# RWKV state step: three products in one PSUM bank, carried states copied by ACT and DVE

## The chip, the cores and the metric

The kernel runs on one core of one Trainium2 chip. The metric is device time in microseconds of one launch. A core has engines that run side by side, each with its own list of instructions, tied by semaphores: TensorE (PE, with its weight loads shown apart as PEld), VectorE (DVE), ScalarE (ACT), GpSimd (POOL) and SyncE (SP, which here only issues transfers). PE writes its products into PSUM; DVE and ACT read them from there; POOL works on SBUF here.

## The reference, cut to what matters

The program is one layer of a hybrid backbone: adaLN modulation, one input projection, then side by side multi-head latent attention (8 heads) and bidirectional RWKV-7 time mixing (16 heads of 64), one output projection, a post norm, and a SwiGLU FFN with its own post norm. 640 tokens: one prompt of 128 and one sample of 512. The part that the change touches is the scan of RWKV, one per direction and head:

```
def step(S, inp):
    r_t, w_t, k_t, v_t, kk_t, a_t = inp
    sa = jnp.einsum("bhvk,bhk->bhv", S, -kk_t)
    S = S * w_t[:, :, None, :] + sa[..., None] * (kk_t * a_t)[:, :, None, :] \
        + v_t[..., None] * k_t[:, :, None, :]
    return S, jnp.einsum("bhvk,bhk->bhv", S, r_t)
s_fin, ys = lax.scan(step, s0, (to_t(r), to_t(decay), to_t(k), to_t(v), to_t(kk), to_t(a)), reverse=reverse)
```

The state S (64 x 64) of every head is carried through the tokens; ys is the output, s_fin of the prompt a result of its own.

## The kernel before, in words

**The scan in chunks.** The tokens are cut into ten chunks of 64 (C = 64). Inside a chunk the recurrence is solved by a small triangular inverse, and only the states at the chunks' borders are carried. Heads go in 8 pairs (index i), both directions d at once (forward, and backward with the order of the tokens reversed), and the ten chunks in two halves j of five. For one pair and half the steps are `rwkv_prep` (factors such as nk and pr), `rwkv_grams` (products of these, m<-pr,nk, copied by ACT to mab and mrb and by DVE to pr), `inverse` (in its middle t<-m,tc of line 617, its transpose u of line 619, and the copies pm and uf of lines 630 to 632 between the products m<-t,mab and m<-u,pm), and `rwkv_chain`. Beside the inverse and the chain run the decays of the other half or the next pair (m<-xa,lw and others; products nk, ta, ks on DVE), the finishing of the pair before (m<-sg,gw onto y), and all the time the big input projection, whose products acc<-xh,whi fill PE's gaps.

**One step of the chain** (e = 0 to 4, 80 in all). px, four small products of the states sv with pr; ACT copies them to xs (line 873); POOL makes sd, the decayed states (line 883); the outputs of the step before are written into two banks and copied (ACT) or added (DVE) into y; psg, four products of xs with the inverse; ACT and DVE copy its two head halves to zv (lines 894 and 895); pn, up to four products of zv with bk; and on DVE up to four scalar-tensor-tensor operations (lines 905 and 906) that make the next state from pn, dc and sd. At the end of the first half the state that goes on is written to cy ("carry"); the second half starts with a copy of it into its own sv, on POOL (line 845), beside two memsets (lines 843 and 846).

**PSUM.** `mps()` gives a tile of one bank with the tag "m"; three banks rotate under that tag for all the work named above. One bank ("x") is for the modulation, and two tiles of two banks ("acc") for the projection.

**Order.** PE's order in this part is the order in which `Jobs` steps through the generators: each `yield HOP[...]` gives a planned delay from a table, and `Tensor.matmul` counts a cost for each product. Banks and the other engines' instructions don't enter into it. The orders of DVE, ACT and POOL are laid out by a scheduler over the whole program. After 1500 us come the output projection and the FFN (products b<-op,qh, b<-p,qh and others; weights are split into a rounded part qh by ACT, line 1302, and the rest ql by DVE), and in the last part, too, the scheduler decides PE's order.

Of the kernel before, what the change touches and what calls it, by code (L numbers as in the profile page):

```python
# [27 lines left out]
C = 64  # L28
# [130 lines left out]
def step_kernel(ctx: ExitStack, tc: tile.TileContext, a: dict, o: dict, upto: int = 99, npairs: int = NPAIR, dbg=None):  # L159
    nc = tc.nc  # L160
    HOP = dict(HOPS[0])
    V, A, G, DMA = nc.vector, nc.scalar, nc.gpsimd, nc.sync
# [11 lines left out]
    def nm(s):  # L174
        uid[0] += 1
        return f"{s}_{uid[0]}"
# [7 lines left out]
    def rtile(name, n, tag, bufs, dtype=F32):  # L184
        return rp.tile([P, n], dtype, tag=tag, name=nm(name), bufs=bufs)

    def slot(name, dtype=F32):
        return rtile(name, NT, "s", N_S, dtype)
# [16 lines left out]
    def mps():  # L205
        return m_ps.tile([P, 512], F32, tag="m", name=nm("m"))
# [19 lines left out]
    def tt(eng, out, x, y, op):  # L226
        eng.tensor_tensor(out=out, in0=x, in1=y, op=op)  # L227
# [7 lines left out]
    def stt(out, x, s, y, op0, op1):  # L235
        V.scalar_tensor_tensor(out=out, in0=x, scalar=s, in1=y, op0=op0, op1=op1)  # L236
# [295 lines left out]
    def rows(h):  # L532
        return slice(64 * h, 64 * h + 64)
# [4 lines left out]
    def cc(e):  # L538
        return slice(e * C, e * C + C)
# [136 lines left out]
    def nat(d, j):  # L676

        h = j if d == 0 else 1 - j
        return slice(h * HN, h * HN + HN)
# [145 lines left out]
    def rwkv_chain(i, j, sh, u):  # L825

        sv_, zv, bk, mrb, pr, dc, cy = u["sv"], u["zv"], u["bk"], u["mrb"], u["pr"], u["dc"], sh["carry"]

        def lanes(t, h, e):

            return t[rows(h), e: e + 6: 5, h, :]

        def lane2(t, h):
            return t[rows(h), :2 * C].rearrange("p (d v) -> p d v", v=C)

        if j == 0:
            sh["fs"] = rtile("fs", 2 * C, "fs", 2)
            sh["y"] = slot("y")
        for h in range(2):
            if j == 0:  # L840
                for d, e in ((0, 0), (1, 7)):
                    DMA.dma_start(out=sv_[rows(h), e, h, :], in_=a["states"][d, i, rows(h)])
                G.memset(sv_[rows(h), 5, h, :], 0.0)
            else:
                G.tensor_copy(lanes(sv_, h, 0), lane2(cy, h))
                G.memset(sv_[rows(h), 3, h, :], 0.0)
        y = sh["y"]

        def outputs(c):


            pss = [mps()[:, :C] for _ in range(2)]
            ms = (slice(0, C), slice(None, None, -1))
            for d, ps in enumerate(pss):
                for h in range(2):
                    T.matmul(ps[rows(h)], sv_[:, 5 * d + c, h, :], pr[h][:, 5 * d + c, 1, :][:, ms[d]], start=True, stop=False)
            for d, ps in enumerate(pss):
                for h in range(2):
                    T.matmul(ps[rows(h)], zv[rows(h), 5 * d + c, h, :], mrb[rows(h), 5 * d + c, :][:, ms[d]], start=False, stop=True)
            for d in range(2):  # L860
                yc = y[:, nat(d, j)][:, cc(c if d == 0 else 4 - c)]
                if j == 0:
                    A.copy(yc, pss[d])
                else:
                    tt(V, yc, pss[d], yc, ALU.add)

        for e in range(5):
            px = mps()
            for d in range(2):
                for h in range(2):  # L870
                    T.matmul(px[rows(h), cc(d)], pr[h][:, 5 * d + e, 0, :], sv_[:, 5 * d + e, h, :], start=True, stop=True)
            xs = rtile("xs", 2 * C, "xs", 2)
            A.copy(xs, px[:, :2 * C])

            to = [AFTER[j, d][e] for d in range(2)]
            ds = [d for d in range(2) if to[d]]
            n = len(ds)
            es = slice(5 * ds[0] + e, 5 * ds[-1] + e + 1, 5)
            dv = slice(ds[0] * C, ds[-1] * C + C)
            sd = rtile("sd", 2 * C, "xs", 2)  # L880
            for h in range(2):
                rh = rows(h)
                tt(G, sd[rh, dv].rearrange("p (d v) -> p d v", v=C), sv_[rh, es, h, :],
                   dc[rh, es].unsqueeze(2).broadcast_to([C, n, C]), ALU.mult)

            if e:
                outputs(e - 1)
            else:
                yield HOP["x"]
            psg = mps()  # L890
            for d in range(2):
                for h in range(2):
                    T.matmul(psg[rows(h), cc(d)], u["u"][rows(h), cc(5 * d + e)], xs[rows(h), cc(d)], start=True, stop=True)
            A.copy(lanes(zv, 0, e), lane2(psg, 0))
            V.tensor_copy(lanes(zv, 1, e), lane2(psg, 1))
            yield HOP["s"]
            pn = mps()
            for d in ds:
                for h in range(2):
                    T.matmul(pn[rows(h), cc(d)], bk[:, 5 * d + e, h, :], zv[:, 5 * d + e, h, :], start=True, stop=True)  # L900
            for h in range(2):
                rh = rows(h)
                for d in ds:
                    q = 5 * d + e
                    dst = sv_[rh, q + 1, h, :] if to[d] == "next" else (cy if to[d] == "carry" else sh["fs"])[rh, cc(d)]
                    stt(dst, pn[rh, cc(d)], dc[rh, q: q + 1], sd[rh, cc(d)], ALU.mult, ALU.add)
            if e < 4:
                yield HOP["p"]
        outputs(4)
        if j == 1:  # L910
            DMA.dma_start(out=o["states"][i], in_=sh["fs"])
# [41 lines left out]
    def rwkv():  # L953
# [19 lines left out]
        for i in range(npairs):  # L973
            for j in range(2):
                yield from rwkv_prep(i, j, sh, u)
                yield from rwkv_grams(u)
                turned = jobs.spawn(rwkv_turned(i, j, sh, u), TURN)
                side = jobs.spawn(beside_second(i, sh) if j else beside_first(i, sh, last), RANK_S)
                u["u"] = yield from inverse(u["mab"])
                yield turned  # L980
                yield from rwkv_chain(i, j, sh, u)
                last = (i, sh)
                yield side
                if side.result:
                    sh, u = side.result
# [305 lines left out]
    def bank():  # L1291
        return b_ps.tile([P, 512], F32, tag="b", name=nm("b"))
# [359 lines left out]
    for n in range(2):  # L1652
        if n:
            ms[0].clear()
        for f in range(KT):
# [9 lines left out]
            ps = bank()  # L1665
# [358 lines left out]
```

## Time and profile before

| what | value |
|---|---|
| time, median of 3 runs | 3491.99 us (3489.88 to 3497.54) |
| profiled execution | 3500.31 us, its span 3498.5 us |
| mean granted clock of TensorE | 0.964 |
| PE busy | 3255.5 us (93%) |
| DVE busy | 2555.3 us (73%) |
| ACT busy | 1480.9 us (42%) |
| POOL busy | 1070.4 us (31%) |

Busy times are sums over the span of one execution. All times of rows further down are from that execution, and are to be set against its 3500.31 us, not against the median. The granted clock is the share of full speed that the throttle left to TensorE: 1.00 in a stretch is 2.4 GHz throughout, 0.50 is 1.2 GHz.

### The profile page before, as it was taken

Reading aid. Unit: us, or ns where it says so; the run is one execution under the profiler, and the core shown is the slowest. Engines: PE = TensorE matmul, PEld = TensorE weight load, DVE = VectorE, ACT = ScalarE, POOL = GpSimd, SP = SyncE. Lnnn points to the kernel's source line nnn. Section 1 sums busy time; section 2 is a strip of 40 time slices with the busy share of each in tenths; the row PEclk is TensorE's granted clock in tenths of the full one; section 3 lists DMA queues with packets and bytes.
Section 4 is the critical chain, followed back from the end, with each engine's and each line's share of the span. In section 5 each row is a group of like instructions: output and inputs, shape, how many; then the busy total and the mean of one; then the engine's idle time right before and its main releaser. Section 6 shows DMA issues by size and latency. Waiting matters only on the chain. (4 is left out here: it accounts for less than half of the span.)

```text
span 3498.5 us, 71287 instructions
## 1 busy us (share of the span) xinstructions
PE 3255.5 (93%) x27538; PEld 2961.4 (85%) x27538; DVE 2555.3 (73%) x4562; ACT 1480.9 (42%) x3115; POOL 1070.4 (31%) x1106
## 2 busy tenths in 40 slices
PE   7988998999999689999979999999999999999987
PEld 4677676777877578899979999999999999999886
DVE  1356766776766676468688888888888888778798
ACT  1144443443443454455454444444444444334334
POOL 0021222122122132102164444444444442212245
PEclk9998999999999899999999999999999999999997
DMA  8754444444211211085434443444443478776743
GB/s 300 240 175 137 142 147 139 161 160 139 66 61 59 72 34 36 31 270 179 142 116 144 155 136 127 134 132 138 133 128 125 144 252 293 255 250 207 256 128 108
DMA packets 289717, 529.06 MB, mean 151 GB/s; under 512 B 31008, under 2 KB 83680, under 8 KB 289376
## 3 DMA queue, kind: packets, MB, share of 16 engines
q1 hardware_dynamic: 289376, 524.49, 45.3%
q8 instruction: 216, 3.54, 0.4%
q14 instruction: 125, 1.02, 0.1%
HBM read 429.65 MB, written 93.09 MB: 149 GB/s over the span
## 5 line engine op out<-in xcount | busy, mean ns | idle before, releaser
L227 DVE TENSOR_TENSOR ql<-raw,qh 128x512 fp32r<-128x512 f32 (+1 forms) x1136 | 930.6, 833 | 263.6 <-ACT qh L1302 242.5
L1302 ACT CAST qh<-raw 128x512 fp32r<-128x512 f32 (+1 forms) x1136 | 660.2, 588 | 913.2 <-PE b L113 777.8
L227 POOL TENSOR_TENSOR raw<-raw,raw 128x512 f32<-128x512 f32 (+1 forms) x288 | 394.4, 1371 | 849.6 <-DVE ql L227 662.2
L113 PE MATMUL b<-t,qh 128*128 128x320 f32 x2816 | 621.7, 310 | 8.6 <-ACT qh L1302 7.3
L113 PE MATMUL b<-op,qh 128*128 128x320 f32 x2464 | 545.9, 315 | 18.2 <-DMA op<-hd 18.0
L113 PEld LDWEIGHTS b<-t,qh 128*128 128x128 f32 x2816 | 471.5, 188 | 10.1 <-ACT qh L1302 8.1
L113 PE MATMUL b<-p,qh 128*128 128x320 f32 x2112 | 468.2, 310 | 0.0
L113 PE MATMUL b<-t,ql 128*128 128x320 f32 x1408 | 435.3, 310 | 6.4 <-DVE ql L227 6.2
L113 PEld LDWEIGHTS b<-op,qh 128*128 128x128 f32 x2464 | 417.9, 192 | 24.6 <-issue 12.3
L113 PE MATMUL b<-op,ql 128*128 128x320 f32 x1232 | 375.3, 316 | 20.1 <-DVE ql L227 20.0
L113 PEld LDWEIGHTS b<-p,qh 128*128 128x128 f32 x2112 | 355.2, 189 | 0.2 <-ACT qh L1302 0.2
L113 PE MATMUL b<-p,ql 128*128 128x320 f32 x1056 | 328.5, 311 | 8.5 <-DVE ql L227 8.5
L113 PEld LDWEIGHTS b<-t,ql 128*128 128x128 f32 x1408 | 264.4, 188 | 8.8 <-DVE ql L227 8.8
L113 PEld LDWEIGHTS b<-op,ql 128*128 128x128 f32 x1232 | 232.4, 191 | 28.5 <-DVE ql L227 28.0
L113 PE MATMUL b<-mh,qh 128*128 128x320 f32 x1024 | 231.0, 315 | 6.4 <-ACT qh L1302 6.2
L113 PE MATMUL acc<-xh,whi 128*128 128x320 f32 x928 | 233.3, 334 | 3.3 <-ACT P L1165 2.5
L113 PE MATMUL acc<-xl,whi 128*128 128x320 f32 x928 | 235.5, 336 | 0.0
L113 PE MATMUL acc<-xh,wlo 128*128 128x320 f32 x928 | 234.3, 335 | 0.0
L227 DVE TENSOR_TENSOR raw<-raw,raw 128x512 f32<-128x512 f32 (+1 forms) x288 | 217.6, 768 | 12.7 <-POOL raw L227 10.8
L113 PEld LDWEIGHTS b<-p,ql 128*128 128x128 f32 x1056 | 199.3, 189 | 11.2 <-DVE ql L227 11.2
L264 ACT CAST whi<-raw 128x512 fp32r<-128x512 f32 (+1 forms) x156 | 94.9, 608 | 232.8 <-PE acc L113 143.8
L113 PEld LDWEIGHTS b<-mh,qh 128*128 128x128 f32 x1024 | 175.4, 192 | 7.6 <-ACT qh L1302 6.8
(331 smaller groups left out, 5686.1 us busy)
## 6 DMA issues: line engine op xcount, KB each, us to landing
wm<-in_w_mod_dram SPq DMA_DIRECT2D x64, 1024.0 KB, 5.3
op<-hd SPq DMA_DIRECT2D x154, 320.0 KB, 5.7
raw<-in_w_gate_dram SPq DMA_DIRECT2D x188, 256.0 KB, 2.7
raw<-in_w_up_dram SPq DMA_DIRECT2D x188, 256.0 KB, 2.9
raw<-in_w_down_dram SPq DMA_DIRECT2D x224, 192.0 KB, 2.8
raw<-in_w_in_dram SPq DMA_DIRECT2D x132, 256.0 KB, 2.7
wm<-in_w_mod_dram SPq DMA_DIRECT2D x64, 512.0 KB, 6.2
raw<-in_w_out_dram SPq DMA_DIRECT2D x128, 256.0 KB, 3.0
```

What stands on the lines that cost most here:

```text
L113: self.eng.matmul(out, lhsT, rhs, start=start, stop=stop)
L227: eng.tensor_tensor(out=out, in0=x, in1=y, op=op)
L264: A.copy(hi, r)
L1302: A.copy(hi, x)
```

## The change

Two edits in `rwkv_chain`. The three products of a step, px, psg and pn, are now three column ranges (128 each) of one bank, taken once at the head of the step, where each took a bank of its own before. And the copy of the carried state goes to ACT for the first head of a pair and to DVE for the second, where POOL made both.

```
@@ -842,7 +842,7 @@
             else:
-                G.tensor_copy(lanes(sv_, h, 0), lane2(cy, h))
+                (A.copy, V.tensor_copy)[h](lanes(sv_, h, 0), lane2(cy, h))
                 G.memset(sv_[rows(h), 3, h, :], 0.0)
@@ -865,12 +865,13 @@
         for e in range(5):
-            px = mps()
+
+            px, psg, pn = (ps[:, k * 2 * C: k * 2 * C + 2 * C] for ps in [mps()] for k in range(3))
             for d in range(2):
                 for h in range(2):
                     T.matmul(px[rows(h), cc(d)], pr[h][:, 5 * d + e, 0, :], sv_[:, 5 * d + e, h, :], start=True, stop=True)
             xs = rtile("xs", 2 * C, "xs", 2)
-            A.copy(xs, px[:, :2 * C])
+            A.copy(xs, px)
@@ -887,14 +888,12 @@
-            psg = mps()
             for d in range(2):
...
             yield HOP["s"]
-            pn = mps()
             for d in ds:
```

PE's order in the RWKV part stays. What its instructions wait for in a step is shown by these rows of PE, with their waits, of one step of the chain in the second half of a pair (pr and sv give the outputs, xs and uf psg, zv and bk pn; acc is the projection). Before:

```order
L113 MATMUL m_9648<-pr_8953,sv_9143 64x64 [waits DVE_49]
L113 MATMUL m_9648<-pr_8954,sv_9143 64x64
L113 MATMUL m_9649<-pr_8953,sv_9143 64x64 [waits DVE_49]
L113 MATMUL m_9649<-pr_8954,sv_9143 64x64
L113 MATMUL m_9648<-mrb_8986,zv_9144 64x64 x2
L113 MATMUL m_9649<-mrb_8986,zv_9144 64x64 x2
L113 MATMUL m_9660<-xs_9643,uf_166 64x64 [waits Activation_49]
...
L113 MATMUL m_9679<-zv_9144,bk_9145 64x64 [waits Activation_49]
L113 MATMUL m_9679<-zv_9144,bk_9145 64x64 [waits DVE_49]
L113 MATMUL m_9679<-zv_9144,bk_9145 64x64 x2
```

And the same rows with the change:

```order
L113 MATMUL m_9668<-pr_8873,sv_9063 64x64 [waits PE_49]
L113 MATMUL m_9668<-pr_8874,sv_9063 64x64
L113 MATMUL m_9669<-pr_8873,sv_9063 64x64 [waits PE_49]
L113 MATMUL m_9669<-pr_8874,sv_9063 64x64
L113 MATMUL m_9668<-mrb_8906,zv_9064 64x64 x2
L113 MATMUL m_9669<-mrb_8906,zv_9064 64x64 x2
L113 MATMUL m_9658<-xs_9663,uf_166 64x64 [waits Activation_49]
...
L113 MATMUL m_9658<-zv_9064,bk_9065 64x64 [waits DVE_49]
L113 MATMUL m_9658<-zv_9064,bk_9065 64x64 x3
```

The outputs' two banks were waited for by way of DVE, and now by way of PE itself; over the program pr,sv has 144 waits on PE alone, where it had 90. The first product of zv and bk waited for ACT (48 times) or for DVE and ACT (31 times) and the second for DVE; now the first waits for DVE, 79 times.

DVE's order moves in a few places beside the inverse. The first is at 976 us of the trace (t and u belong to the inverse of the next half; nb, ta, nk and ks to the factors of that half; uf is the inverse's result; wlo is a split weight of the projection). Before:

```order
L236 SCALAR_TENSOR_TENSOR nb_11119<-ta_10990,kk_10047 128x320 x2
L227 TENSOR_TENSOR t_1849_11066<-m_11067,tc_10843 128x320
L233 TENSOR_SCALAR ta_10990<-ta_10990,ka_h,ka_c 128x640
L236 SCALAR_TENSOR_TENSOR nk_11513<-nb_11119,ld_10989 64x10x64 x2
L619 STREAM_TRANSPOSE u_1851_11109<-t_1849_11066 128x320
L227 TENSOR_TENSOR ta_10990<-ta_10990,k_10043 128x320 x2
L632 COPY uf_166<-u_1851_11109 32x10x32 x2
L227 TENSOR_TENSOR wlo_11178<-raw_11062,whi_11177 128x512
L227 TENSOR_TENSOR nk_11513<-ta_10990,ld_10989 64x10x64 x2
```

With the change:

```order
L236 SCALAR_TENSOR_TENSOR nb_11019<-ta_10890,kk_9957 128x320 x2
L233 TENSOR_SCALAR ta_10890<-ta_10890,ka_h,ka_c 128x640
L236 SCALAR_TENSOR_TENSOR nk_11403<-nb_11019,ld_10889 64x10x64 x2
L227 TENSOR_TENSOR ta_10890<-ta_10890,k_9953 128x320 x2
L227 TENSOR_TENSOR t_1749_10966<-m_10967,tc_10743 128x320
L227 TENSOR_TENSOR nk_11403<-ta_10890,ld_10889 64x10x64 x2
L619 STREAM_TRANSPOSE u_1751_11009<-t_1749_10966 128x320
L236 SCALAR_TENSOR_TENSOR ks_10077<-ks_10077,vec,r_9951 128x640
L632 COPY uf_166<-u_1751_11009 32x10x32 x2
```

The product t moves behind five instructions, its transpose u behind two more, and uf behind ks. ACT there copies uf before pm, where it copied pm, then a weight, then uf.

The second place on DVE is at 842 us, with the same names, one and a half pairs earlier. Before:

```order
L233 TENSOR_SCALAR ta_9281<-ta_9281,ka_h,ka_c 128x640
L227 TENSOR_TENSOR t_1577_9357<-m_9358,tc_9139 128x320
L236 SCALAR_TENSOR_TENSOR nk_9802<-nb_9410,ld_9280 64x10x64
L227 TENSOR_TENSOR ta_9281<-ta_9281,k_8329 128x320 x2
L236 SCALAR_TENSOR_TENSOR nk_9802<-nb_9410,ld_9280 64x10x64
L619 STREAM_TRANSPOSE u_1579_9400<-t_1577_9357 128x320
L227 TENSOR_TENSOR nk_9802<-ta_9281,ld_9280 64x10x64 x2
L632 COPY uf_166<-u_1579_9400 32x10x32 x2
L236 SCALAR_TENSOR_TENSOR ks_8440<-ks_8440,vec,r_8327 128x640
```

With the change:

```order
L233 TENSOR_SCALAR ta_9201<-ta_9201,ka_h,ka_c 128x640
L236 SCALAR_TENSOR_TENSOR nk_9712<-nb_9330,ld_9200 64x10x64
L227 TENSOR_TENSOR ta_9201<-ta_9201,k_8259 128x320 x2
L236 SCALAR_TENSOR_TENSOR nk_9712<-nb_9330,ld_9200 64x10x64
L227 TENSOR_TENSOR t_1497_9277<-m_9278,tc_9059 128x320
L227 TENSOR_TENSOR nk_9712<-ta_9201,ld_9200 64x10x64 x2
L619 STREAM_TRANSPOSE u_1499_9320<-t_1497_9277 128x320
L236 SCALAR_TENSOR_TENSOR ks_8370<-ks_8370,vec,r_8257 128x640
L632 COPY uf_166<-u_1499_9320 32x10x32 x2
```

Here t moves behind four instructions, u behind two, uf behind ks. Elsewhere in this part DVE, ACT and POOL have single neighbours swapped; in the last 180 us all engines' orders differ by some slots.

## Rows read from the trace of the kernel before

**Rows 1.** The page, section 1: busy us (share of span) xinstructions.

```profile
PE 3255.5 (93%) x27538; PEld 2961.4 (85%) x27538; DVE 2555.3 (73%) x4562; ACT 1480.9 (42%) x3115; POOL 1070.4 (31%) x1106
```

**Rows 2.** Stretches: window, length, busy PE, PEld, DVE, ACT, POOL; PEclk, DMA share, GB/s.

```profile
200.00:1500.00 1300.00, 1155.88 (x13786) 959.49 (x13786) 848.79 (x1869) 572.44 (x1445) 300.92 (x493) 0.94 0.32 106
3300.00:3450.00 150.00, 132.64 (x848) 125.19 (x846) 140.44 (x256) 61.27 (x130) 75.38 (x61) 0.96 0.45 144
```

**Rows 3.** Groups by line, 0 to 1560 us: xcount | busy, mean ns | idle before, releasers.

```profile
L113 PE MATMUL m<-pr,nk 64*128 64x128 f32 x640 | 60.7, 297 | 29.3 <-DVE nk L227 9.0 <-DVE y L227 9.0 <-POOL sv L846 8.3
...
L113 PE MATMUL m<-pr,sv 128*64 128x64 f32 x640 | 35.0, 223 | 0.0
...
L895 DVE COPY zv<-m 64x128 f32<-64x128 f32 x80 | 23.6, 295 | 63.6 <-ACT zv L894 63.0
...
L894 ACT COPY zv<-m 64x128 f32<-64x128 f32 x80 | 20.8, 260 | 29.7 <-PE m L113 28.5
...
L845 POOL COPY sv<-cy 64x128 f32<-64x128 f32 x16 | 7.1, 445 | 0.9
```

**Rows 4.** Waits, 200 to 1500 us: engine line <- releaser: us in total, times, longest.

```profile
ACT mab L811 <- PE m L113: 70.4, 31, 6.0
...
DVE zv L895 <- ACT zv L894: 63.0, 67, 2.9
...
DVE pr L227 <- ACT mab L811: 44.7, 35, 3.3
...
PE m L113 <- DVE y L227: 24.0, 17, 2.1
...
PE m L113 <- DVE zv L895: 5.0, 8, 1.3
```

**Rows 5.** Line 845: who waited for it, us and times.

```profile
  POOL P L233: 2.8, 1
  POOL t L227: 2.6, 1
```

**Rows 6.** Timeline near 842 us, DVE and PE: start, us, instruction xcount.

```profile
842.47 0.48 DVE L227 TENSOR_TENSOR t<-m,tc 128x320 f32<-128x320 f32 x1
...
845.93 0.51 DVE L619 STREAM_TRANSPOSE u<-t 128x320 f32<-128x320 f32 x1
...
845.08 0.82 PE L113 MATMUL m<-t,mab 32*32 32x32 f32 x40
```

**Rows 7.** Timeline near 976 us, DVE, PE and ACT.

```profile
976.40 0.48 DVE L227 TENSOR_TENSOR t<-m,tc 128x320 f32<-128x320 f32 x1
...
979.00 0.51 DVE L619 STREAM_TRANSPOSE u<-t 128x320 f32<-128x320 f32 x1
...
980.32 1.80 DVE L632 COPY uf<-u 32x320 f32<-32x320 f32 x2
...
982.85 1.86 DVE L227 TENSOR_TENSOR nk<-ta,ld 64x640 f32<-64x640 f32 x2
...
978.97 0.82 PE L113 MATMUL m<-t,mab 32*32 32x32 f32 x40
...
981.68 0.82 PE L113 MATMUL m<-u,pm 32*32 32x32 f32 x40
...
979.83 0.86 ACT L630 COPY pm<-m 32x320 f32<-32x320 f32 x2 [3.05 <-PE m L113]
...
981.25 0.92 ACT L631 COPY uf<-u 32x320 f32<-32x320 f32 x2
```

**Rows 8.** Last stage, 3300 to 3498 us: a wait of PE, DVE's splits.

```profile
PE b L113 <- DVE ql L227: 19.0, 22, 1.7
...
L227 DVE TENSOR_TENSOR ql<-raw,qh 128x384 fp32r<-128x384 f32 x98 | 63.4, 657 | 5.1 <-ACT qh L1302 5.1
```

**Rows 9.** PE's stall at 807 us, and the stretch behind it.

```profile
806.99 2.04 PE L113 MATMUL m<-pr,nk 64*128 64x128 f32 x14 [1.71 <-DVE y L227]
...
807.00:820.00 13.00, 13.00 (x90) 10.95 (x90) 7.97 (x13) 9.06 (x22) 1.26 (x1) 0.87 0.46 148
```

More of the change, by code (lines that the diff above doesn't have):

```diff
@@ L844, in rwkv_chain @@
             else:
-                G.tensor_copy(lanes(sv_, h, 0), lane2(cy, h))
+                (A.copy, V.tensor_copy)[h](lanes(sv_, h, 0), lane2(cy, h))
                 G.memset(sv_[rows(h), 3, h, :], 0.0)
@@ L867, in rwkv_chain @@
         for e in range(5):
-            px = mps()
+            px, psg, pn = (ps[:, k * 2 * C: k * 2 * C + 2 * C] for ps in [mps()] for k in range(3))
             for d in range(2):
@@ L872, in rwkv_chain @@
             xs = rtile("xs", 2 * C, "xs", 2)
-            A.copy(xs, px[:, :2 * C])
+            A.copy(xs, px)
             to = [AFTER[j, d][e] for d in range(2)]
@@ L889, in rwkv_chain @@
                 yield HOP["x"]
-            psg = mps()
             for d in range(2):
@@ L896, in rwkv_chain @@
             yield HOP["s"]
-            pn = mps()
             for d in ds:
```

## The prediction

> **What bounds the kernel.** I read the page first: TensorE (PE) is busy 93% of the span, VectorE (DVE) 73%, and no other engine half of it [rows 1]. The page's chain of waits is no help (its shares round to 0%), so I went to the busy time by stretch [rows 2]. The reader is to see two stages with different limits. In the RWKV and attention part, 200 to 1500 us, PE is idle for 1300 − 1155.88 = 144 us, in many short waits. In the last 150 us before the drain DVE is busy 140.44 of 150 us and PE 132.64: there DVE sets the pace. The change edits only the first of these, but a scheduler lays out DVE, ACT and POOL for the whole program, and its new order differs in the last stage too. So the sum needs two kinds of terms: what the edited lines cost, and what the reordering costs.
>
> For the RWKV part I read the groups by line [rows 3], then the waits [rows 4], and at the two places where DVE's order changes most the timeline [rows 6, 7]. PE's order is written out by a model of hops that knows nothing of banks or copies, and it doesn't change before the last stage.
>
> **The three products in one bank.** The banks taken in a step go from 5 (px, two of outputs, psg, pn) to 3, in 8 pairs × 2 halves × 5 = 80 steps. Three things could come of it.
> - Waits for a bank could become fewer. PE waits 24.0 us in 17 places for a DVE write of y [rows 4], the write that frees a bank which outputs filled; 9.0 of it stands before the gram products pr·nk [rows 3]. But these waits come at the end of a chain, where the last two banks taken are those of outputs(4), before and now, and with three banks in rotation the second new product still meets the first of these. I take 0; the other end is all 24.0 us gained.
> - The first zv·bk product now waits for DVE's copy of zv at once. Before, it waited for ACT's copy and the second product for DVE's (the order rows of PE show one such step). PE stood there 5.0 us, 8 times [rows 4]. What is lost is at most the one product that used to go ahead, 223 ns by its like [rows 3], so 8 × 0.22 = 1.8 us; as the second had to wait in any case, I take a quarter, +0.5 us.
> - Outputs' products pr·sv now have a wait on PE itself 144 times, before 90. The products waited for stand 11 to 29 instructions earlier, and the 90 of before leave no idle time on the row of pr·sv (0.0) [rows 3]. I take 0; if each of the 54 new ones cost a product, it would be 54 × 0.223 = +12 us.
>
> Within a step nothing that ran side by side is put in a row: psg needs xs, and pn needs both copies of zv, by their data. DVE's copy of zv does wait for ACT's copy out of the same bank, 63.0 us in 67 places [rows 4], but in the kernel before, where psg had a bank of its own; the change leaves that as it is.
>
> The Trainium skill (Perfetto Trace Analysis, "Matmuls") says that independent groups of products should rotate through different banks, so that emptying one overlaps the next group's products. By that rule this change is a step back; no run here shows yet what a side job loses by it (rival 3).
>
> **The carried states.** POOL loses 16 copies of 445 ns, 7.1 us [rows 3]. Who waited for them were two instructions of POOL itself, 2.8 and 2.6 us [rows 5], and POOL is busy 300.92 of 1300 us here [rows 2]. The 8.3 us that PE waited before pr·nk are put down to POOL's memset of line 846 [rows 3], which stays and stood ahead of the copies. So POOL's relief gives 0; the other end is 2.8 + 2.6 = 5.4 us gained. ACT and DVE get 8 copies each. No row has them there; the nearest are the copies of zv, of the same shape but out of PSUM, 260 ns on ACT and 295 ns on DVE [rows 3], and POOL's own 445. That makes 8 × 0.26 = 2.1 us and 8 × 0.295 = 2.4 us, at most 3.6 each. On ACT the copy stands before the copies mab, which wait 70.4 us for PE in 31 places; on DVE it stands before the pr<-m products, which wait 44.7 us for mab in 35 [rows 4]. Both are covered: 0. With that cover gone at every pair, mab comes 0.26 us later 8 times, +2 us on the way to the inverse.
>
> **DVE's new order beside the inverse.** In each of the 16 halves the product t<-m,tc, its transpose u and the copies uf stand between the products nk and ta of the same half. In two halves t now comes later.
> - At 976.40 us [rows 7]: between t and the copies uf (980.32) stood ta, two nk, the transpose u and two ta. All but u (0.51) now go ahead of t, so t ends at about 980.32 − 0.51 = 979.8. PE began t·mab at 978.97 without waiting; with some 0.1 for the signal it will begin at 979.9, +0.9. The transpose then follows two nk<-ta (1.86) and ends at 979.8 + 1.9 + 0.5 = 982.2. ACT, whose order here turns from pm, whi, uf to uf, pm, then copies uf (0.92) and pm (0.86), until 984.0; u·pm, due at 981.68 + 0.9 = 982.6, stands until then in the worst case (+1.4), and until the first half of pm in the better one (+1.0). Together about +2.1.
> - At 842.47 us [rows 6]: the three groups of nk and ta that stood between t and u now go ahead of t, so t ends where u began, 845.93. PE began t·mab at 845.08: +0.9. The later transpose costs less here, since more filler stands before u·pm in PE's order; I take +0.4. Together +1.3.
>
> In the other direction single DVE instructions change places so that the inverse's own come one earlier, at about two places that matter; each by some 0.5 us like t or u [rows 6, 7], −1.0. For the stage that is 2.1 + 1.3 − 1.0 = +2.4. If other filler takes it up, it is 0; if the stalls also bring the clock down, more (rival 2).
>
> **The last stage.** DVE's work is the same in total, and so is PE's, but in some of the last loops the splits ql stand one slot ahead of the norm's operations. PE waits 19.0 us in 22 places for ql, 1.7 at the longest [rows 8]. DVE is idle 150 − 140.44 = 9.6 us between 3300 and 3450 [rows 2], which is all that a better order can give; a worse one might add a longest wait in each of six loops, 6 × 1.7 = +10. One slot is a ql of 0.66 us [rows 8], and with two or three waits met I take −1.5.
>
> **Sum.** 0.5 + 2.4 − 1.5 = +1.4 us on the profiled execution of 3500.31 us (its span 3498.5 and 1.8 around it), so 3501.7. That execution lies 8.3 us above the median of the runs shown, 3491.99, which is what the change is measured by; the terms are the same there, and I forecast 3493.4 us. Less than about 0.2%, 7 us, a measurement of this kernel can't tell from no change.
>
> **Rivals.**
> 1. *The freed banks let PE start earlier* (faster). For it: 24.0 us of waits for y [rows 4], and 160 allocations fewer. Against: banks go by rotation, and a gram or a decay meets outputs' banks in either kernel. If half of the waits go, 3493.4 − 12 = 3481; all of them, 3469.
> 2. *The late t brings the clock down* (slower). The place is t·mab at 845 and 979 us. Behind a stall of 1.71 us at 807 us the granted clock is 0.87 over 13 us [rows 9], against 0.94 in the whole stage [rows 2]: 13 × 0.13 = 1.7 us. It decides once a new stall comes near that length; mine are 0.9 to 1.4. For it: the half's whole chain starts later and has no slack of its own. Two stalls with 1.7 each, the 1.0 and the 1.5 not given back, and as much again where ACT's later copies meet the next step: 1.4 + 3.4 + 2.5 + 3 = +10, 3502.
> 3. *One bank held for a whole step starves the rest* (slower). Outputs and all side jobs then share two banks for most of a step. Price: one wait for y of 24.0/17 = 1.4 us more in half of the 16 halves, 8 × 1.4 = +11, 3505. Against it: outputs are emptied well before their bank comes round, and PE's waits name the same instructions as before nearly everywhere.
> 4. *Only POOL's hidden time is moved* (same): 3492.
>
> **How the numbers follow.** Forecast and rival 4 together 0.60. Rival 1, with a larger gain in the last stage, 0.19, nearly all of it faster by over 0.2%. Rival 2 0.12 and rival 3 0.09, the slower 0.21. The forecast's own range is 3487 to 3499. To hold 8 in 10 it reaches down to 3482, the lighter half of rival 1, and up to 3503, which takes in rival 2.
>
> **What the changed profile would show.** Right: the copies sv<-cy at some 0.3 us on ACT and DVE, with nobody waiting for them; PE's wait for y still near 24 us; the wait for zv at 5 to 6 us; t·mab near 845 and 979 us with about 0.9 us of idle time behind DVE's t, and u·pm near 982 us behind ACT's pm; PE's wait for ql somewhat under 19.0. Wrong: a wait for y at half or less (rival 1); a new stretch of low clock behind those two places (rival 2); new waits for y, fs or sv before px, xs·uf or the outputs (rival 3). Above all the forecast is wrong if PE's idle time between 200 and 1500 us moves by more than 7 us from 144.

## The result and the profile after

The changed kernel takes 3501.16 us (median of 20 runs, 3493.56 to 3510.66), the kernel before 3494.06 (20 runs, 3487.27 to 3503.04): ratio 1.0018, 95% interval 1.0009 to 1.0026. That is slower by 6.3 us (3 to 9), where +1.4 was forecast. Single executions of one kernel spread over 16 to 17 us, and the two profiled ones lie the wrong way round: 3497.22 us here (span 3495.4), 3500.31 before. So no total of one profile can show this difference; places in it can.

The busy times, in answer to [rows 1, 2]: the page's section 1, then the two stretches (busy PE, PEld, DVE, ACT, POOL; clock).

```profile
PE 3249.1 (93%) x27538; PEld 2956.6 (85%) x27538; DVE 2553.4 (73%) x4570; ACT 1483.7 (42%) x3123; POOL 1062.0 (30%) x1090
```

```profile
200.00:1500.00 1300.00, 1153.46 (x13801) 956.02 (x13802) 848.95 (x1880) 576.55 (x1457) 294.58 (x477) 0.94 0.33 106
3300.00:3450.00 150.00, 131.13 (x841) 124.56 (x840) 142.52 (x258) 62.22 (x130) 75.72 (x63) 0.96 0.45 139
```

POOL has lost its copies and ACT has gained some. In the first stretch PE and its weight loads are busy 2.4 and 3.5 us less, in the second DVE is busy 2.1 us more. PE's idle time between 200 and 1500 us, the sign by which the forecast was to stand or fall above all, is 1300 − 1153.46 = 146.5 us, only 2.4 more than before: between these two executions it doesn't show the loss. The groups that the two edits touch, in answer to [rows 3]:

```profile
L113 PE MATMUL m<-pr,nk 64*128 64x128 f32 x640 | 61.2, 299 | 29.4 <-DVE nk L227 9.0 <-DVE y L227 8.8 <-POOL sv L846 8.3
...
L113 PE MATMUL m<-pr,sv 128*64 128x64 f32 x640 | 35.2, 224 | 0.0
```

The gram products wait as long as before (29.4 and 29.3), for the same three; the outputs' products, with their 54 new waits on PE, still have no idle time before them. The copies of the carried state, line 845 (duration minimum, median, maximum in ns; the last lines would say who waited, and nobody did):

```profile
L845 ACT COPY sv<-cy x8: 298/299/300, 334.5 to 1303.5; 64x128 f32<-64x128 f32 x8
...
L845 DVE COPY sv<-cy x8: 220/222/222, 338.2 to 1307.4; 64x128 f32<-64x128 f32 x8
```

The waits of PE, 200 to 1500 us, in answer to [rows 4]:

```profile
PE m L113 <- DVE y L227: 24.7, 18, 2.1
PE m L113 <- DVE tc L600: 13.8, 3, 6.3
PE m L113 <- DVE t L227: 13.0, 6, 3.7
...
PE m L113 <- DVE zv L895: 6.5, 8, 1.6
```

Two of these waits in the kernel before:

```profile
PE m L113 <- DVE tc L600: 17.4, 3, 9.0
...
PE m L113 <- DVE t L227: 6.5, 4, 3.7
```

The wait for y is where it was (24.0), that for zv 1.5 us longer, that for tc 3.6 us shorter, and one has doubled: DVE's t, 13.0 us, which was 6.5. The two places where t comes late, in answer to [rows 6, 7] (start, us, instruction, in brackets the idle time before it):

```profile
846.79 0.49 DVE L227 TENSOR_TENSOR t<-m,tc 128x320 f32<-128x320 f32 x1
...
847.43 0.82 PE L113 MATMUL m<-t,mab 32*32 32x32 f32 x40 [2.86 <-DVE t L227]
```

```profile
982.58 0.48 DVE L227 TENSOR_TENSOR t<-m,tc 128x320 f32<-128x320 f32 x1
...
983.21 1.27 PE L113 MATMUL m<-t,mab 32*32 32x32 f32 x40 [3.30 <-DVE t L227]
984.41 0.90 PE L113 MATMUL acc<-xh,whi 128*128 128x320 f32 x2
985.11 0.73 PE L113 MATMUL acc<-xl,whi 128*128 128x320 f32 x2
...
987.91 1.12 PE L113 MATMUL m<-u,pm 32*32 32x32 f32 x40
```

PE stands 2.86 and 3.30 us, where it stood 0 and 0.9 each was forecast. (The two places are one pair apart, not one and a half as the section on the change has it.) Behind the second stall two of the projection's products take 0.73 us, where they take 0.46 at full clock (from 979.16 us): the granted clock has fallen to half from 983 to 988 us. The stretch 983 to 995 has 0.76 in the mean. A low stretch follows the first stall too, 0.72 from 848 to 854 us. In the kernel before both windows have 1.00.

```profile
848.00:854.00 6.00, 6.00 (x79) 4.10 (x74) 3.70 (x7) 2.48 (x6) 1.29 (x2) 0.72 0.15 44
983.00:988.00 5.00, 4.79 (x56) 4.43 (x58) 4.48 (x7) 1.87 (x5) 3.12 (x4) 0.50 0.01 3
983.00:995.00 12.00, 11.21 (x141) 9.96 (x142) 6.38 (x12) 5.90 (x14) 4.10 (x5) 0.76 0.12 27
```

### The profile page after: what moved, and what is told of

The parts are those of the page before. It is cut to its first block, busy times and chain, and to the rows that moved or that the text cites. A ratio compares the mean times of both kernels' runs of the same rounds, so it can differ in the third digit from the quotient of the medians.

```text
span 3495.4 us, 71264 instructions
## 1 busy us (share of the span) xinstructions
PE 3249.1 (93%) x27538; PEld 2956.6 (85%) x27538; DVE 2553.4 (73%) x4570; ACT 1483.7 (42%) x3123; POOL 1062.0 (30%) x1090
## 4 chain that ended last, share of the span: by engine, by line
PE 55%; DVE 7%; issue 2%; ACT 2%; DMA 2%; POOL 1%; SPq 0%; ACTq 0%; DVEq 0%; POOLq 0%
PE b L113 48%; PE acc L113 4%; PE m L113 2%; DVE ql L227 1%; DVE z L227 1%; DMA op<-hd 1%; PE x L113 1%; POOL z L227 1%; DVE ns L227 0%; DVE z L236 0%; ACT z L239 0%; DVE raw L227 0%; PE acc L117 0%; DVE smx L1163 0%; DVE pr L227 0%
```

## The experiments

A trick makes the experiments clean: a scheduler lays out the engines' orders, but an edge can be added that sets issue order alone, without a wait. Where a kernel is "held in an order", each engine's instructions are chained so:

```
def in_order(tc, nc):
    dep = mybir.DependencyInfo(mybir.DependencyClass.NoSync, mybir.DependencyReason.DATA)
    for eng, runs in ORDER.items():
        ins = [x for x in nc.cur_bb.bb.instructions if str(x.engine).endswith("." + eng) and ...]
        for run in runs:
            for b_, a_ in zip(run, run[1:]):
                tc.add_manual_dep(ins[a_], ins[b_].name, dep, reason="issue_after")
```

ORDER holds the wanted order as numbers of the instructions as they are traced. The theories: the bank costs (waits), the copies cost (cover gone), or the order that comes with the change costs, beside the inverse, in the attention part or at the end.

All were timed in five rounds against the kernel before, each with 7 to 12 runs of its own; "before" stands for its median in the same series.

| run | median us | before | ratio, 95% interval |
|---|---|---|---|
| copies only (e1) | 3494.63 | 3492.15 | 1.0001, 0.9990 to 1.0012 |
| bank only (e2) | 3502.48 | 3492.15 | 1.0029, 1.0019 to 1.0040 |
| change, old order (e3) | 3494.11 | 3492.15 | 1.0004, 0.9994 to 1.0014 |
| before, new order (e4) | 3503.75 | 3492.15 | 1.0030, 1.0020 to 1.0041 |
| change, old order to 1140 us (e5) | 3494.04 | 3493.30 | 1.0001, 0.9991 to 1.0010 |
| change, old order from 1500 us (e6) | 3500.13 | 3493.30 | 1.0016, 1.0007 to 1.0025 |
| change, second place old (e7) | 3494.05 | 3493.30 | 1.0001, 0.9991 to 1.0010 |
| change, first place old (e8) | 3496.34 | 3493.30 | 1.0009, 0.9999 to 1.0018 |
| t and pm first (e9) | 3498.32 | 3492.40 | 1.0017, 1.0006 to 1.0028 |
| t, pm and y first (e10) | 3490.32 | 3492.40 | 0.9994, 0.9984 to 1.0004 |
| before, y first (e11) | 3488.25 | 3494.80 | 0.9975, 0.9965 to 0.9985 |
| change, old to 1140, y first (e12) | 3490.58 | 3494.80 | 0.9987, 0.9976 to 0.9998 |

**One part alone.** Copies only:

```
-                G.tensor_copy(lanes(sv_, h, 0), lane2(cy, h))
+                (A.copy, V.tensor_copy)[h](lanes(sv_, h, 0), lane2(cy, h))
```

> Only the copies of the carried states go to ACT and DVE; the three products keep a bank each, and every engine's other instructions stand in the order of before. If the copies are covered (the forecast's term, 0): ratio to before 0.9995 to 1.0005, that is within 2 us, nobody waits for sv<-cy, and POOL loses 7 us of work for nothing. If the new copies hold up mab and the pr products at every pair (the other end, 0.26 us 8 times and more): +2 to +5 us, and the wait of DVE's pr for ACT's mab grows by 2 us or more.

Bank only (the rest of the change's diff, with that line as before):

> Only the three products share a bank; POOL copies the carried states as before. The scheduler's order on DVE, ACT and POOL is that of the changed kernel, copies aside. If the loss of 7 us lies in the bank or in the order that comes with it: +5 to +8 us, ratio 1.0014 to 1.0023. If it lies in the copies: within 2 us of before.

Measured: the copies alone 1.0001, the bank alone 1.0029 (its interval overlaps that of the whole change). The copies bring no other instruction out of its order; the bank alone brings the whole reordering. So bank or order.

**Bank against order.** The changed kernel held in the order of before, and the kernel before held in the order that the bank brings:

```
 e3: after.py  + in_order(tc, nc)    # ORDER: that of the copies alone, the order of before
 e4: before.py + in_order(tc, nc)    # ORDER: that of the bank alone
```

> Both edits, but all engines' instructions are held in the order that they have in the kernel before (by edges that set issue order alone and add no wait; the copies stand where they stand in the changed kernel). If the order is what costs: back to within 2 us of before. If sharing a bank costs by itself (54 more waits of PE on itself, fewer banks for the side jobs, the wait of zv,bk): +5 to +8 us as in the changed kernel, with the loss in PE's idle time between 200 and 1500 us.

> The kernel before, banks and POOL copies as they were, but held in the order that the shared bank brings on DVE, ACT, POOL, SP and, in the last part, PE. If the order costs: +5 to +8 us. If the bank costs: within 2 us of before. By the forecast's terms for the order (+2.4 in the RWKV part, -1.5 at the end) it would be +1.

Measured: 1.0004 and 1.0030. The loss goes with the order and not with the bank, in both directions; what is left to bank and copies together is −2 to +5 us. The second place in e3 (first fence), and both places in e4 (second and third):

```profile
973.13 0.48 DVE L227 TENSOR_TENSOR t<-m,tc 128x320 f32<-128x320 f32 x1
...
973.76 0.82 PE L113 MATMUL m<-t,mab 32*32 32x32 f32 x40 [0.16 <-DVE t L227]
```

```profile
847.89 0.82 PE L113 MATMUL m<-t,mab 32*32 32x32 f32 x40 [2.12 <-DVE t L227]
```

```profile
983.32 0.82 PE L113 MATMUL m<-t,mab 32*32 32x32 f32 x40 [1.20 <-DVE t L227]
987.58 0.24 PE L113 MATMUL m<-u,pm 32*32 32x32 f32 x2 [1.48 <-ACT pm L630]
```

With the bank and the copies of the change but the old order, PE waits 0.16 us for t here, and not at all at the first place. With the banks of before but the new order it waits 2.12 at the first place, and at the second 1.20 for t and another 1.48 for ACT's pm, which the new order puts behind uf.

**Which part of the order.** The changed kernel with pieces of the old order put back: everything up to about 1140 us; everything after 1500 us; the second place alone (13 instructions of DVE, 5 of ACT, at 976 us of the trace of before); the first place alone (11 and 3, at 842 us).

```
 O["DVE"][1271:1284], O["Activation"][924:929] = those of before      # e7, second place
 O["DVE"][1066:1077], O["Activation"][776:779] = those of before      # e8, first place
```

> The changed kernel with DVE, ACT and POOL held in the order of before up to about 1140 us (the inverses and chains of RWKV); the attention part and the last stage keep the changed kernel's order. If the late products t at two inverses are the cost: back to within 2 us of before (ratio 0.9995 to 1.0006). If the cost lies in the attention part or in the last stage: +5 to +8 us as the changed kernel.

> The changed kernel with only the part after 1500 us held in the order of before (DVE, ACT, POOL, SP and PE in the last stage). If the late products t are the cost: no change against the changed kernel, +5 to +9 us over before. If the last stage's order is the cost: within 2 us of before. The forecast's term for the last stage would make it 1.5 us slower than the changed kernel.

> The changed kernel with one place alone put back: 13 instructions of DVE and 5 of ACT around the product t at 976 us stand as in before. From PE's idle time there (3.3 us behind t in the changed kernel, and the start of the next chain 4 to 5 us late): back by 4 to 5 us, +2 to +3 us over before. If several places or the whole order matter: +5 us or more.

> The changed kernel with the place at 842 us alone put back (11 instructions of DVE, 3 of ACT). PE's idle time behind t there was 2.9 us and the next chain starts about 2 us late: back by 2 us, +5 us over before. If a low clock behind the stall doubles it: back by 4 us.

Measured: 1.0001, 1.0016, 1.0001, 1.0009. With the old order up to 1140 us the loss is gone; with the old order at the end alone it stays. Of the two places the second alone brings back all that can be measured (by the ratios 6 us, where 4 to 5 were expected), the first alone about 3 (2 expected). With intervals of 3 us and more to each side, the times don't say how much belongs to each. The traces say more, by the time from the first product m<-sv,pr of one chain to that of the next, with the place between the two. Across the second place, in the trace of before and in that of the changed kernel:

```profile
914.15 0.45 PE L113 MATMUL m<-sv,pr 128*64 128x64 f32 x8
...
984.38 0.45 PE L113 MATMUL m<-sv,pr 128*64 128x64 f32 x8
```

```profile
917.82 0.45 PE L113 MATMUL m<-sv,pr 128*64 128x64 f32 x8
...
990.92 0.45 PE L113 MATMUL m<-sv,pr 128*64 128x64 f32 x8
```

That is 70.2 and 73.1 us. In the five traces with the late t there (the changed kernel, e2, e4, e6, e8) it is 72.8 to 73.5, in five with the old order (before, e1, e3, e5, e7) 64.8 to 70.2: in the mean 5.6 us more. Across the first place it is 69.8 to 70.4 us (the changed kernel, e2, e4, e6, e7) against 67.1 to 69.1 (before, e1, e3, e5, e8): 2.1 us more.

The section on the change leaves out a third stretch, at 1157 to 1177 us, where several of DVE's instructions change places. It keeps its new order in e5, so it costs nothing that can be measured. PE's wait for tc goes with it: 16.2 to 17.4 us in the six traces with the old order there (before, e1, e3, e9, e10, e11), 13.8 to 15.0 in the eight with the new one.

**A version that beats both.** The kernel before has a late t of its own, at 439 us (3.7 us of PE's 6.5), and a bank freed late. The first try puts t and its transpose ahead of ta and nk in three halves and pm ahead of uf or D in six:

```
 DVE: nb nb ta nk ta ta nk t ...  ->  nb nb t ta nk u ta ta nk ...
 ACT: uf uf pm pm                 ->  pm pm uf uf
```

> The changed kernel in the order of before, and in three halves (those at 439, 842 and 1110 us of the trace of before) the product t and its transpose u go ahead of ta, nk and the rest on DVE; in six halves ACT copies pm before uf, or before D. If a late t costs what the two places showed: PE's waits for t (6.5 us in the kernel before, 3.7 of it at 439 us) fall to 1 us or less, those for pm (3.5) to 1 or less, and the kernel is 5 to 9 us faster than before, ratio 0.9974 to 0.9986. If what is won there is lost at the next wait for DVE (the wait for tc at 1179 us grows by as much): within 2 us of before.

Measured: 1.0017, slower by 6 us; the expected gain is refuted, though the waits for t did fall. Four of PE's waits, 200 to 1500 us:

```profile
PE x L113 <- DMA wm<-in_w_mod_dram: 10.3, 4, 3.9
...
PE m L113 <- ACT xs L874: 9.0, 8, 3.4
...
PE m L113 <- DVE zv L895: 8.5, 8, 1.9
...
PE m L113 <- DVE t L227: 1.1, 2, 0.6
```

t costs 1.1 us where it was 6.5, but the wait for the modulation's weights rose from 4.4 to 10.3, that for xs from 6.7 to 9.0 and that for zv from 5.0 to 8.5. Against e3, which has both edits and the order of before, they rose from 0.8, 4.8 and 8.0, so little of the wait for zv comes from this reordering. At 439 us one sees how: DVE copies uf at 442.62 us, and in the kernel before at 442.73, since nk, ta, wlo and ks all still stand ahead of it, and PE, there earlier, now waits for wlo and uf instead (first fence; the second is from the kernel before).

```profile
441.87 0.56 PE L113 MATMUL acc<-xh,wlo 128*128 128x320 f32 x2 [0.39 <-DVE wlo L227]
443.08 0.70 PE L113 MATMUL m<-xs,uf 64*64 64x64 f32 x8 [0.66 <-DVE uf L632]
...
442.62 0.67 DVE L632 COPY uf<-u 32x320 f32<-32x320 f32 x2
```

```profile
442.73 0.67 DVE L632 COPY uf<-u 32x320 f32<-32x320 f32 x2
```

Why it is slower than before, and not just no faster, isn't settled by this.

The second try adds the last outputs to y before the fourth pr<-kk product, not after it:

```
 DVE: pr<-kk pr<-kk pr<-kk pr<-kk y<-m,y y<-m,y  ->  pr<-kk pr<-kk pr<-kk y<-m,y y<-m,y pr<-kk     # 7 places
```

> As the kernel before it, and at the end of each second half DVE adds the last outputs to y before the fourth pr<-kk product rather than after it (seven places). These adds free the bank for which the gram products pr,nk wait 1.0 to 1.7 us each (9.0 us in all). If that wait really ends with the adds: PE's wait for y falls by 5 to 8 us, and the kernel gains another 5 to 10 us over the one without it, counting the stretches of low clock behind these stalls. If the grams then wait for the third or fourth pr product instead: no gain, and PE's wait is put down to pr.

Measured: 0.9994, 8 us below e9 by medians of one series. So the swap was tried without t and pm, on the kernel before and on the change with the old order up to 1140 us:

> The kernel before, banks, copies and all, in its own order but for seven swaps on DVE: at the end of each second half the two adds of the last outputs to y go ahead of the fourth pr<-kk product. PE's stalls before the gram products there, 0.9 to 1.7 us each, should fall by 1.07 us each, as they did in the run with t and y first (1.64 to 0.57). Seven times that is -7 us, ratio about 0.998, if nothing behind takes it up. If the next wait takes it up, as happened with t first: within 2 us of before.

> The changed kernel with the order of before up to 1140 us and the same seven swaps. The bank and the copies cost nothing by the runs so far, so the time should be that of the kernel before with the swaps, within 2 us: ratio to before about 0.998 if the swaps gain, 1.000 if not. If the shared bank makes the grams' wait different (the bank that they meet belongs to a step), the gain differs by more than 3 us between the two.

Measured: 0.9975 (0.9965 to 0.9985), 8.7 us faster than before by the ratio (5 to 12; the medians lie 6.6 apart), and 0.9987 (0.9976 to 0.9998). The first has the lowest ratio of all versions: before's banks and copies with seven swaps. The place of [rows 9] in e11, and the stretch behind it:

```profile
805.07 1.13 PE L113 MATMUL m<-pr,nk 64*128 64x128 f32 x14 [0.64 <-DVE y L227]
```

```profile
806.00:815.00 9.00, 8.97 (x68) 7.04 (x66) 6.11 (x11) 7.34 (x18) 1.26 (x1) 1.00 0.48 151
```

The stall is 0.64 us instead of 1.71, and no stretch of low clock follows: the clock is 1.00 there, and the 14 products take 1.13 us, not 2.04. PE's whole wait for y is down:

```profile
PE m L113 <- DVE y L227: 18.3, 16, 2.1
```

That is 5.7 of the 24.0 us gone, and not seven times 1.07: four stalls fell by 1.06 or 1.07 us, one by 0.40, and one of 0.96 is gone.

The clock in one place of two traces could be chance, but the other traces bear it out. In the eleven traces without the swaps, the nine us from the end of a stall of 1.63 to 1.71 us before these products have a granted clock of 0.81 or less in 31 of 44 places; behind the stalls of 0.92 to 1.28 us it is 1.00 in all 22, and behind those of 0.57 to 0.87 that e10, e11 and e12 have left in all 15. At 0.81 nine us lose 1.7, so an estimate from these rows is 4 × 31/44 × 1.7 = 4.8 us of clock beside the 5.7 us of waits, together in the upper part of the measured 5 to 12. The two versions differ by 0.0012, within their intervals; that the bank makes the difference isn't shown.

## Why the prediction came out as it did

**The edited lines: right.** The bank costs and gains nothing that can be measured, as forecast (0.5 us); the wait for y stayed at 24.7, that for zv rose to 6.5 (5 to 6 forecast), the waits on PE itself show no idle time. Rival 1 fell with the wait for y, rival 3 with e3. The copies cost nothing (e1), and nobody waited for them. The Trainium skill's rule that groups should rotate through banks (Perfetto Trace Analysis, "Matmuls") speaks of independent groups; e3, with three dependent ones in one bank, shows no cost.

**DVE's order beside the inverse: the right place, the wrong size.** This is the step that failed. It said +2.4, made of 0.9 at each t·mab, 1.2 and 0.4 behind them, less 1.0 for swaps that help; with the old order put back there, the loss of some 6 us goes, and the two places measure 5.6 and 2.1 us in the traces, where 2.1 and 1.3 were forecast. The fault was to read slack from one execution. In the trace of before PE came to t·mab at 845.08 and 978.97 us, 2.1 us after t had ended (842.95 and 976.88), because it ran at half clock just ahead of both places: 0.53 in 834 to 845 us, 0.57 in 969 to 979, in the same view as [rows 2]:

```profile
834.00:845.00 11.00, 11.00 (x189) 9.82 (x174) 6.68 (x14) 3.46 (x7) 0.84 (x1) 0.53 0.31 107
969.00:979.00 10.00, 10.00 (x192) 8.41 (x191) 6.39 (x11) 3.51 (x8) 0.00 (x0) 0.57 0.13 43
```

In other executions it is not so. In e1, which has DVE's order of before, the clock is 1.00 in the ten us ahead of the second place, and t·mab begins 0.15 us after t has ended:

```profile
962.70:972.70 10.00, 8.04 (x197) 6.41 (x195) 5.35 (x11) 4.00 (x9) 1.53 (x1) 1.00 0.12 43
```

```profile
972.07 0.48 DVE L227 TENSOR_TENSOR t<-m,tc 128x320 f32<-128x320 f32 x1
...
972.70 0.82 PE L113 MATMUL m<-t,mab 32*32 32x32 f32 x40
```

Nine traces have the old order at this place. From the end of t to the start of t·mab they show 2.1 us where the clock of the five us ahead is 0.64 (before, e11), 0.9 where it is 0.81 (e5, e9), and 0.15 to 0.19 where it is 0.96 to 1.00 (e1, e3, e7, e10, e12). The last five have no slack: 0.15 us also lies between the end of t and a t·mab that waited for it (847.28 to 847.43 us in the changed kernel), and in e3 PE waits 0.16 us as it is. The new order makes t 3.1 us later (it starts 3.94 us after nb in the changed kernel, 0.81 in the one before), and that delay is then nearly all PE's: 0.16 + 3.1 is 3.3, and 3.30 was measured here, 2.86 at the first place. The other traces with the late t have 1.20 to 3.30 us at the second place and 2.12 to 2.48 at the first.

So the 2.1 us that I took off twice were not slack of the kernel but time lost to the clock in that run. Against that one trace the forecast comes near, 73.1 − 70.2 = 2.9 us across the second place and 70.4 − 69.1 = 1.3 across the first; against the mean of five traces it is short by 3.5 and 0.8. Of the swaps that help, put at −1.0, no run shows a size by itself; the shorter wait for tc may be part of it.

**Rival 2, the low clock behind the new stall,** was put at +10 and 0.12, and is nearer to the measured +6.3 than the forecast is. I let it begin at stalls near 1.71 us and took mine for 0.9 to 1.4; they were longer than that. Its sign came: low stretches follow both places in the changed kernel's trace, behind the second 12 × 0.24 = 2.9 us of clock. In the twelve us from the start of t·mab at the second place, four of the five traces with the late t have 0.61 to 0.77, behind stalls of 2.78 to 3.30 us; e4, with 1.20, has 1.00, and so have all nine with the old order. But across the place e4 takes as long as the others (73.5 us), so how much of the loss the low clock makes stays open.

**The last stage: not borne out.** −1.5 was forecast for it. With the old order put back there the changed kernel doesn't measurably change (1.0016 against 1.0018), and PE's wait for ql is as long as it was, 19.0 us [rows 8], in fewer places:

```profile
PE b L113 <- DVE ql L227: 18.8, 17, 2.8
```

A gain of 1.5 us lies within the intervals, so the runs neither show nor exclude it.

**The range and the sign.** 3501 lies within 3482 to 3503, but outside the forecast's own 3487 to 3499: the range holds it because it was drawn out to take in rival 2, not because the sum was right. "Same within 0.2%" is what the ratio 1.0018 says, though its interval shows it slower, so twenty runs of each do tell a change of under 7 us.

## What to carry to other kernels

An edit of buffers or banks can be free by itself and still cost, because the scheduler puts other instructions elsewhere: compare the orders, and hold the order fixed to part the two. Slack read from one profile is worth only what the granted clock in front of it is worth: ask when the waiting engine would come at full clock, or read the place in several executions. And seven swaps of two short adds gave 8.7 us, while t put ahead, with uf and wlo still as late, gave none: look at what follows a wait on the same queue before taking it away. That this is the reason for the difference is argued from two cases, not shown.

## What the runs showed of the hardware that was not expected

The copy of a carried state, 64x128 in SBUF, takes 222 ns on DVE and 299 on ACT, against 445 on POOL in the mean; out of PSUM the same shape took 295 and 260 [rows 3], so for this shape ACT is the faster from PSUM and DVE the faster from SBUF. And the wait on PE's own earlier product, 144 times, shows no idle time at all (224 ns for a product, 223 before).
